# A hybrid decoder layer: transposes of the probabilities ahead of the filling products, later sums of h, and the cache copy in sixteen pieces

## The chip, the cores and the metric

The kernel runs on one core of one Trainium2 chip. The metric is the device time of one execution in microseconds, lower being better; the time of the kernel before is the median of three runs.

## The reference

One decoder layer with three parallel branches is computed in float32 for a prompt of 1024 tokens and, with the same weights, for 8 sample tokens that each have caches. The model's width is 1024.

```python
z = x @ w_in                                   # one projection for all branches and gates
xr, yr, q, k, v, xq, g = jnp.split(z, SPLIT_IDX, axis=-1)
a_out = rg_lru(causal_conv(xr)) * gelu(yr)     # branch a: a linear recurrence
s_out = swa(q, k, v, sinks)                    # branch s: window of 128, 16 query heads, 4 kv heads of 64
c_out = mem_attn(xq, mem_k, mem_v)             # branch c: 256 memory tokens, 4 heads of 256
merged = sum(gates[:, :, n] * (br @ w_branch[n]) for n, br in enumerate((a_out, s_out, c_out)))
h = layer_norm(ALPHA * x + merged @ w_out)
gt, up = jnp.split(h @ w_gate_up, 2, axis=-1)
y = layer_norm(ALPHA * h + (silu(gt) * up) @ w_down)
```

Outputs are y for prompt and samples, the new states of convolution and recurrence, the memory keys and values, and the window caches; the samples' window caches are the old ones shifted by one row, with the new row at the end.

## The kernel before, in words

**Precision.** TensorE multiplies in a reduced float32 format, so each operand is split into a high part, cast on ScalarE (ACT), and a low remainder, subtracted on VectorE (DVE): `split`, lines 80 and 81. A product is then three matmuls (high by high, high by low, low by high; `mm3`, lines 114 to 116) into one PSUM bank. The attention values take two, because there the stationary operand holds both parts side by side.

**Layout and stages.** Activations lie with channels on the 128 partitions and 1032 tokens (1024 and 8) along the free dimension. The tokens are taken in three chunks of 388, 386 and 258 columns (`CH`). In order of time the stages are: `project` (to some 630 us), which computes z by a scheme of seven products in place of eight per pair of weight tiles (`fast_quarter` prepares a weight quarter, `fast_product` multiplies), with the recurrence and the samples' memory attention as side work; `mem_attention` (to some 800 us); `windows` (to some 1030 us); the rest of the branch products and `out_proj` with the first layer norm; `ffn`, whose gate and up products again use the seven products for 20 of 22 column tiles (`gated_step`); and `down` with the second layer norm.

**PSUM.** The eight banks are handed out by tag, two each: `mm`, `s`, `t` and `o`.

**Filling products.** The products of the branches a and c with `w_branch` (tiles `bra` and `brc`, 24 matmuls each) depend on nothing in the attention stages. `fill(1)` traces the next one of them at places chosen by hand, so that TensorE has work while ACT and DVE do a softmax. In `mem_attention` every other half step has a head's key/value projection (`mem_kv`) at that place.

**Window stage.** There are 32 steps, 4 key/value heads by 8 blocks of 128 tokens. `win_scores` makes the scores of four query heads (`bs`, lines 573 and 574, eight matmuls into two banks `s`), masks them and takes the maximum on DVE (line 577), the exponentials on ACT (581), the reciprocal on DVE (582), and multiplies on DVE, POOL and ACT (588 and 586). The values are one step behind: `win_values` of the step before transposes the probabilities on TensorE (`bt`, line 598, four transposes for each of two key blocks), splits the transposed ones (`bph` and `bpl`), multiplies them with the values (`bo`, lines 603 and 604) and stores the result through `bob`. The branch s reads it back later.

**What sets the order.** The program is traced in Python, and a scheduler orders each engine's instructions ahead of time: of those that are ready by its own clock it takes the one that was traced first. Each engine then runs its list in that order and waits at each instruction for what it needs. `issue_after(x)` adds an edge: what is traced in its block on the engine of x is listed behind x. So where a call stands in the source is its priority.

**Sums of h.** For the seven products of `ffn`, `combine` makes sums and differences of blocks of h on DVE and splits them, in three parts for each half of the columns. The last two parts of the second half are traced in phase `ph5b`, beside the weight quarters of the first unit: one part behind the low remainder of the first weight quarter (`last_low`), one behind that of the second.

**Cache copies.** All but one row of the samples' window caches is copied within device memory, 1016 KB for keys and as much for values. Both copies are issued on SyncE's queue (SP) during the seven-product units, behind the weight loads of units 14 and 15. Copies of h back into the residual tiles (516 KB each) are issued in the same way in units 4 to 11. SP issues all DMAs of the kernel.

**First down products.** `down` begins with the two column tiles that were kept on the chip (tile `dk`): eight output tiles, four column ranges each, whose PSUM banks alternate between the tags `mm` and `s`. The last seven-product unit uses the same tags.

Of the kernel before, what the change touches and what calls it, by code (L numbers as in the profile page):

```python
# [18 lines left out]
P = 128  # L19
# [3 lines left out]
NB = 8  # L23
# [7 lines left out]
F_KEPT = (20, 21)  # L31
F_UNITS = F_KEPT + tuple(range(2, 20))
F_DOWN = ((0, 7), (14, 6), (7, 7))
F_CACHE = {8: ("o_swk", "cwk"), 9: ("o_swv", "cwv")}
NORM_AT = (0, 3)
LATE_AT = {4: 2, 5: 3, 6: 5}
CENTER_AT = (2, 4, 5)
# [2 lines left out]
QN = T // 4  # L40
# [19 lines left out]
class Builder:  # L60
# [428 lines left out]
            out.append(p)  # L489
        return out  # L490

    def mem_values(self, h, half, ps, mv):
        nc = self.nc
        pt = [self.bank("t", f"cpt{h}_{half}_{kk}") for kk in range(2)]
        for pr, p in enumerate(ps):
            for u in range(2):
                for kk in range(2):
                    nc.tensor.transpose(pt[kk][:, (pr * 2 + u) * P:(pr * 2 + u + 1) * P],
                                        p[:, u * 256 + kk * P:u * 256 + (kk + 1) * P], self.ident)
        pp = []  # L500
        for kk in range(2):
            hi = self.ph.tile([P, 512], F32R, tag="pt", name=f"cph{h}_{half}_{kk}", bufs=4)
            lo = self.ph.tile([P, 512], F32R, tag="pt", name=f"cpl{h}_{half}_{kk}", bufs=4)
            self.split(hi, lo, pt[kk])
            pp.append((hi, lo))
        for j in range(2):
            o = self.bank("o", f"co{h}_{half}_{j}")
            self.mm3(o, [((mv[kk][0][:, j * P:(j + 1) * P], mv[kk][1][:, j * P:(j + 1) * P]), pp[kk])
                         for kk in range(2)])
            ob = self.ph.tile([P, 512], F32, tag="ob", name=f"cob{h}_{half}_{j}", bufs=2)  # L510
            nc.scalar.copy(ob, o)
            nc.sync.dma_start(self.scr["c"][:, 2 * h + j, half * 512:(half + 1) * 512], ob)

    def mem_attention(self, fill):

        self.load_mem()
        kv = [None] * 4
        fill(6)
        kv[0] = self.mem_kv(0)
        last = None  # L520
        for n in range(8):
            h, half = n // 2, n % 2
            ps = self.mem_scores(h, half, self.mem_queries(h, half), kv[h][0])
            if half == 0 or h == 3:
                fill(1)
            else:
                kv[h + 1] = self.mem_kv(h + 1)
            if last:
                self.mem_values(*last)
            last = h, half, ps, kv[h][1]  # L530
            if n in DEC_AT:
                (self.dec_win_scores, self.dec_win_softmax, self.dec_win_values)[DEC_AT.index(n)]()
        fill(1)
        self.mem_values(*last)


    def win_load(self, kv):
# [50 lines left out]
                (nc.gpsimd if g else nc.vector).tensor_scalar_mul(pg[g], pg[g], r)  # L588
        return pg

    def win_values(self, kv, ops, b, pg):
        nc = self.nc
        nk, vs = len(range(max(b - 1, 0), b + 1)), ops[2]
        ov = self.bank("o", f"bo{kv}_{b}")
        for kk in range(nk):
            pt = self.bank("t", f"bt{kv}_{b}_{kk}")
            for g in range(4):
                nc.tensor.transpose(pt[:, g * P:(g + 1) * P], pg[g][:, kk * P:(kk + 1) * P], self.ident)
            hi = self.ph.tile([P, 512], F32R, tag="pt", name=f"bph{kv}_{b}_{kk}", bufs=4)
            lo = self.ph.tile([P, 512], F32R, tag="pt", name=f"bpl{kv}_{b}_{kk}", bufs=4)  # L600
            self.split(hi, lo, pt)
            v = vs[:, max(b - 1, 0) + kk, :]
            nc.tensor.matmul(ov, v, hi, start=kk == 0, stop=False)
            self.last_mm = nc.tensor.matmul(ov, v, lo, start=False, stop=kk == nk - 1).ins
        for i in range(2):
            ob = self.ph.tile([64, 256], F32, tag="ob", name=f"bob{kv}_{b}_{i}", bufs=4)
            o = ov[:, i * 256:(i + 1) * 256]
            nc.scalar.copy(ob, o[64:128, :])
            nc.vector.tensor_add(ob, o[0:64, :], ob)
            dst = self.scr["s"][:, 2 * kv + i, b * P:(b + 1) * P].rearrange("(e d) t -> d e t", e=2)  # L610
            nc.sync.dma_start(dst, ob.rearrange("p (e t) -> p e t", e=2))

    def windows(self, fill):

        self.mask = self.ph.tile([P, 256], F32, tag="mask", name="mask", bufs=1)
        self.nc.sync.dma_start(self.mask, self.io["cst"][:, P:P + 256])
        nxt, last = self.win_load(0), None
        fill(2)
        for kv in range(4):
            ops = nxt  # L620
            for b in range(8):
                pg = self.win_scores(kv, ops, b)
                if last:
                    fill(1)
                    self.win_values(*last)
                last = kv, ops, b, pg
                if b == 4 and kv < 3:
                    nxt = self.win_load(kv + 1)
        fill(1)
        self.win_values(*last)  # L630

    def product(self, step, br, m, c, wb, gate):

# [564 lines left out]
    def ffn(self, h):  # L1198
        nc, io, tc = self.nc, self.io, self.tc

        def gate_up(f, c, wg, wu):
            t0, n = CH[c]
            pg = self.mm_tile(wg, h, c, f"fg{f}_{c}", tag=("t", "s")[c % 2])
            self.norm_step()
            t = self.ph.tile([P, CW], F32, tag="gt", name=f"ft{f}_{c}", bufs=3)[:, :n]
            nc.scalar.activation(t, pg, AF.Tanh, scale=0.5)
            nc.vector.scalar_tensor_tensor(t, t, 1.0, pg, op0=ALU.add, op1=ALU.mult)
            pu = self.mm_tile(wu, h, c, f"fu{f}_{c}")
            last = nc.vector.tensor_mul(t, t, pu).ins
            nc.sync.dma_start(self.scr["f"][:, f, t0:t0 + n], t)  # L1210
            return last

        st, ts, sums = {}, [], []

        def load(f):
            st[f] = self.fast_load(f"f{f}", io["wgu"][f], io["wgu"][NF + f])
            st[f]["load"]((0, 0), (0, 1), (1, 0), (1, 1))

        todo = [(f, i) for f in F_UNITS for i in range(7)]
        with self.phase("ph5a") as self.ph:  # L1220
            h = self.out_proj(h)
            for f in F_DIRECT:
                wg = self.weights(io["wgu"][f], D, f"wfg{f}")
                wu = self.weights(io["wgu"][NF + f], D, f"wfu{f}")
                for c in range(3):
                    last = gate_up(f, c, wg, wu)
                    if (f, c) in ((0, 1), (1, 0)):
                        with tc.issue_after(self.last_half if f == 0 else last):
                            ts.append({})
                            sums.append(self.combine(f, ts[f]))  # L1230
                            for _ in range(3 - 2 * f):
                                next(sums[f])
        g = [[None] * 3 for _ in range(7)]
        with self.phase("ph5b") as self.ph:
            self.w1 = self.ph
            load(F_UNITS[0])
            for k in range(3):
                self.fast_quarter(st[todo[k][0]], todo[k][1])
                if k < 2:
                    with tc.issue_after(self.last_low):  # L1240
                        next(sums[1])
            for k, (f, i) in enumerate(todo):
                j = k // 7
                if i == 1 and j + 1 < len(F_UNITS):
                    load(F_UNITS[j + 1])
                    if 4 <= j < 12:
                        with tc.issue_after(self.last_load):
                            nc.sync.dma_start(self.M[j - 4], self.scr["h"][:, j - 4, :])
                    if j in (14, 15):
                        name, cache = F_CACHE[j - 6]  # L1250
                        with tc.issue_after(self.last_load):
                            nc.sync.dma_start(io[name][:, 0:P - 1, :], io[cache][:, 1:P, :])
                if k + 3 < len(todo):
                    v, q = todo[k + 3]
                    self.fast_quarter(st[v], q)
                self.gated_step(st[f], i, ts, f)
                if f == F_UNITS[-1] and i in (2, 4, 6):
                    for e in {2: range(4), 4: (4, 5), 6: (6,)}[i]:
                        g[e] = self.load_gated(F_DOWN[0][0] + e, self.S[1][e])
        with self.phase("ph5c") as self.ph:  # L1260
            self.down(g)

    def down(self, g):
# [7 lines left out]
        for m in range(KT):  # L1271
            w = self.weights(io["wdn"][m][:, cols(F_KEPT[0], 2)], 2 * P, f"wdk{m}")
            for th in range(2):
                for p in range(2):
                    ps = self.bank(("mm", "s")[p], f"dk{m}_{th}{p}")[:, :QN]
                    o = HT + QN * p
                    self.mm3(ps, [(w[j], tuple(a[:, o:o + QN] for a in self.S[0][2 * j + th])) for j in range(2)])
                    add(m, HT * th + QN * p, QN, ps)
# [244 lines left out]
```

## Time and profile before

| | before |
|---|---|
| median of 3 runs | 1940.3 us (1939.17 to 1942.13) |
| profiled execution | 1941.22 us |
| its span | 1939.4 us |
| granted TensorE clock | 0.998 |
| TensorE busy, matmuls | 1907.9 us, 98% |
| VectorE busy | 1369.9 us, 71% |
| ScalarE busy | 995.8 us, 51% |
| memory read and written | 194.75 MB and 70.03 MB |

The profile is that of one execution. PE is TensorE's matmuls, PEld its weight loads, which overlap with them; POOL is GpSimd and SP SyncE. A wait is listed under the engine and line that waited and the engine and tile that released it. Rows of the timeline give the start in us, the duration in us, engine, line, operation, and the tiles that it writes and reads; "x8" means that so many rows are merged. The groups give the busy time in us and the mean of one in ns, and behind the second bar the idle time just before.

### The profile page before, as it was taken

The numbers are of one execution on the slowest core, as the hardware profiler recorded it, in microseconds if no ns is written. First come the engines' busy times: TensorE is split into PE (matmuls) and PEld (weight loads), VectorE is DVE, ScalarE is ACT, GpSimd is POOL, SyncE is SP. The second block draws the span as 40 slices with busy tenths as digits, with TensorE's granted clock in tenths as the row PEclk, the third lists the DMA queues.
The fourth block names the chain that finished last, engine by engine and source line by source line (L and its number), as shares of the span: only waits on it lengthen the run. The fifth ranks groups of instructions, "written<-read, shape, count | busy, mean of one in ns | idle before, by whom it ended". The sixth has DMA issues, their size and how long they took to land.

```text
span 1939.4 us, 37218 instructions
## 1 busy us (share of the span) xinstructions
PE 1907.9 (98%) x14245; PEld 1878.5 (97%) x14245; DVE 1369.9 (71%) x2922; ACT 995.8 (51%) x2164; POOL 74.4 (4%) x125
## 2 busy tenths in 40 slices
PE   8999999999999999999999999999999999999997
PEld 8999999999999999988999999999999999999997
DVE  8998889878776655388886558885666656734557
ACT  6666765656665555398774234643333333412224
POOL 0010000100000000021210000000000000000000
PEclk9999999999999999999999999999999999999999
DMA  5554554465233976657525242212333222623202
GB/s 205 179 181 155 172 178 140 159 217 178 80 137 115 304 223 210 166 165 208 148 64 180 88 154 74 94 62 88 110 104 102 101 88 77 186 74 119 83 10 88
DMA packets 154850, 265.14 MB, mean 137 GB/s; under 512 B 18624, under 2 KB 76816, under 8 KB 154640
## 3 DMA queue, kind: packets, MB, share of 16 engines
q1 hardware_dynamic: 154672, 262.76, 42.4%
q8 instruction: 112, 1.84, 0.4%
q14 instruction: 66, 0.54, 0.1%
HBM read 194.75 MB, written 70.03 MB: 137 GB/s over the span
## 4 chain that ended last, share of the span: by engine, by line
PE 84%; ACT 5%; DVE 5%; DMA 4%; issue 2%; SPq 0%; ACTq 0%; DVEq 0%; POOL 0%; POOLq 0%
PE ub L291 4%; PE ub L293 4%; PE ub L292 4%; PE fb L292 4%; PE fb L291 4%; PE fb L293 4%; PE d L115 3%; PE d L116 3%; PE d L114 3%; PE ud L293 2%; PE ud L292 2%; PE ud L291 2%; PE fd L291 2%; PE fd L293 2%; PE fd L292 2%; PE brs L115 2%
## 5 line engine op out<-in xcount | busy, mean ns | idle before, releaser
L581 ACT ACTIVATE bp<-bp,bst 128x257 f32<-128x257 f32 (+1 forms) x128 | 62.7, 493 | 18.2 <-DVE bst L577 18.0
L291 PE MATMUL ub<-th,u_6h 128*128 128x258 f32 x232 | 66.4, 286 | 1.1 <-DVE zb L321 1.1
L293 PE MATMUL ub<-th,u_4l 128*128 128x258 f32 x232 | 65.9, 285 | 0.3 <-DVE u_4l L81 0.3
L291 PE MATMUL ub<-th,u_2h 128*128 128x258 f32 x232 | 66.0, 284 | 0.1
L293 PE MATMUL uc<-th,u_3l 128*128 128x258 f32 x232 | 65.9, 284 | 0.0
L293 PE MATMUL ud<-th,u_1l 128*128 128x258 f32 x232 | 65.9, 284 | 0.0
L293 PE MATMUL ub<-th,u_2l 128*128 128x258 f32 x232 | 65.9, 284 | 0.0
L293 PE MATMUL ud<-th,u_5l 128*128 128x258 f32 x232 | 65.9, 284 | 0.0
L291 PE MATMUL uc<-th,u_3h 128*128 128x258 f32 x232 | 65.7, 283 | 0.0
L293 PE MATMUL ub<-th,u_0l 128*128 128x258 f32 x232 | 65.7, 283 | 0.0
L293 PE MATMUL ub<-th,u_6l 128*128 128x258 f32 x232 | 65.6, 283 | 0.0
L291 PE MATMUL ud<-th,u_5h 128*128 128x258 f32 x232 | 65.6, 283 | 0.0
L291 PE MATMUL ud<-th,u_1h 128*128 128x258 f32 x232 | 65.6, 283 | 0.0
L291 PE MATMUL ub<-th,u_4h 128*128 128x258 f32 x232 | 65.5, 283 | 0.0
L292 PE MATMUL ub<-tl,u_0h 128*128 128x258 f32 x232 | 65.5, 282 | 0.0
L291 PE MATMUL ub<-th,u_0h 128*128 128x258 f32 x232 | 65.4, 282 | 0.0
L292 PE MATMUL ud<-tl,u_1h 128*128 128x258 f32 x232 | 65.3, 282 | 0.0
L292 PE MATMUL ub<-tl,u_2h 128*128 128x258 f32 x232 | 65.3, 282 | 0.0
L292 PE MATMUL uc<-tl,u_3h 128*128 128x258 f32 x232 | 65.3, 282 | 0.0
L292 PE MATMUL ub<-tl,u_4h 128*128 128x258 f32 x232 | 65.3, 282 | 0.0
L292 PE MATMUL ud<-tl,u_5h 128*128 128x258 f32 x232 | 65.3, 282 | 0.0
L292 PE MATMUL ub<-tl,u_6h 128*128 128x258 f32 x232 | 65.3, 281 | 0.0
(828 smaller groups left out, 8052.9 us busy)
## 6 DMA issues: line engine op xcount, KB each, us to landing
ur<-win SPq DMA_DIRECT2D x120, 256.0 KB
urf<-wgu SPq DMA_DIRECT2D x80, 256.0 KB
scr_f<-fo SPq DMA_DIRECT2D x36, 258.0 KB
dck<-cmk SPq DMA_DIRECT2D x32, 256.0 KB
dcv<-cmvT SPq DMA_DIRECT2D x32, 256.0 KB
st<-scr_q SPq DMA_DIRECT2D x32, 256.0 KB
S1L<-scr_f SPq DMA_DIRECT2D x14, 516.0 KB
scr_g<-za SPq DMA_DIRECT2D x12, 516.0 KB
```

The source lines that it names most:

```text
L114: nc.tensor.matmul(ps, sh, mh, start=i == 0, stop=False)
L115: nc.tensor.matmul(ps, sh, ml, start=False, stop=False)
L116: self.last_mm = nc.tensor.matmul(ps, sl, mh, start=False, stop=closes and i == last).ins
L291: mm(sh[:, w], xh, start=opens and k == 0, stop=False)
L292: mm(sh[:, w], xl, start=False, stop=False)
L293: self.last_mm = mm(sl[:, w], xh, start=False, stop=k == 3).ins
L581: nc.scalar.activation(x, x, AF.Exp, bias=st[:, g:g + 1], scale=-1.0, accum_out=st[:, 4 + g:5 + g])
```

## The change

Five things change.

- In `windows`, `win_values` is cut in two. `win_turn` transposes and splits; what is left multiplies and stores. `win_turn` of the step before is traced ahead of `fill(1)`, the rest behind it as now.
- In `mem_attention`, `mem_values` is cut in the same way into `mem_turn` and `mem_values`.
- In `ffn`, both remaining parts of the sums of h are traced behind the low remainder of the second weight quarter.
- The cache copies become sixteen pieces of 127 rows of 256 floats (127 KB), one sample of keys or values each, behind the weight loads of units 3 to 18.
- In `down`, the first products take banks by column half: two in `s`, two in `mm`.

```diff
-F_CACHE = {8: ("o_swk", "cwk"), 9: ("o_swv", "cwv")}
+F_CACHE = (("o_swk", "cwk"), ("o_swv", "cwv"))
...
-    def mem_values(self, h, half, ps, mv):
+    def mem_turn(self, h, half, ps):
         nc = self.nc
         pt = [self.bank("t", f"cpt{h}_{half}_{kk}") for kk in range(2)]
...
             self.split(hi, lo, pt[kk])
             pp.append((hi, lo))
+        return pp
+
+    def mem_values(self, h, half, pp, mv):
+        nc = self.nc
         for j in range(2):
...
             ps = self.mem_scores(h, half, self.mem_queries(h, half), kv[h][0])
+            if last:
+                turned = self.mem_turn(*last[:3])
             if half == 0 or h == 3:
                 fill(1)
             else:
                 kv[h + 1] = self.mem_kv(h + 1)
             if last:
-                self.mem_values(*last)
+                self.mem_values(*last[:2], turned, last[3])
...
+    def win_turn(self, kv, ops, b, pg):
+        nc = self.nc
+        pairs = []
+        for kk in range(len(range(max(b - 1, 0), b + 1))):
             pt = self.bank("t", f"bt{kv}_{b}_{kk}")
             for g in range(4):
                 nc.tensor.transpose(pt[:, g * P:(g + 1) * P], pg[g][:, kk * P:(kk + 1) * P], self.ident)
             hi = self.ph.tile([P, 512], F32R, tag="pt", name=f"bph{kv}_{b}_{kk}", bufs=4)
             lo = self.ph.tile([P, 512], F32R, tag="pt", name=f"bpl{kv}_{b}_{kk}", bufs=4)
             self.split(hi, lo, pt)
+            pairs.append((hi, lo))
+        return pairs
+
+    def win_values(self, kv, ops, b, pairs):
+        nc = self.nc
+        nk, vs = len(pairs), ops[2]
+        ov = self.bank("o", f"bo{kv}_{b}")
+        for kk, (hi, lo) in enumerate(pairs):
             v = vs[:, max(b - 1, 0) + kk, :]
...
                 pg = self.win_scores(kv, ops, b)
                 if last:
+                    turned = self.win_turn(*last)
                     fill(1)
-                    self.win_values(*last)
+                    self.win_values(*last[:3], turned)
...
                 self.fast_quarter(st[todo[k][0]], todo[k][1])
-                if k < 2:
+                if k == 1:
                     with tc.issue_after(self.last_low):
+                        next(sums[1])
                         next(sums[1])
...
-                    if j in (14, 15):
-                        name, cache = F_CACHE[j - 6]
+                    if 3 <= j < 3 + 2 * NB:
+                        name, cache = F_CACHE[(j - 3) % 2]
+                        b = (j - 3) // 2
                         with tc.issue_after(self.last_load):
-                            nc.sync.dma_start(io[name][:, 0:P - 1, :], io[cache][:, 1:P, :])
+                            nc.sync.dma_start(io[name][b, 0:P - 1, :], io[cache][b, 1:P, :])
...
-                    ps = self.bank(("mm", "s")[p], f"dk{m}_{th}{p}")[:, :QN]
+                    ps = self.bank(("s", "mm")[th], f"dk{m}_{th}{p}")[:, :QN]
```

More of the change, by code (lines that the diff above doesn't have):

```diff
@@ L532, in mem_attention @@
                 (self.dec_win_scores, self.dec_win_softmax, self.dec_win_values)[DEC_AT.index(n)]()
+        turned = self.mem_turn(*last[:3])
         fill(1)
-        self.mem_values(*last)
+        self.mem_values(*last[:2], turned, last[3])
     def win_load(self, kv):
@@ L589, in win_scores @@
         return pg
-    def win_values(self, kv, ops, b, pg):
+    def win_turn(self, kv, ops, b, pg):
         nc = self.nc
-        nk, vs = len(range(max(b - 1, 0), b + 1)), ops[2]
-        ov = self.bank("o", f"bo{kv}_{b}")
-        for kk in range(nk):
+        pairs = []
+        for kk in range(len(range(max(b - 1, 0), b + 1))):
             pt = self.bank("t", f"bt{kv}_{b}_{kk}")
@@ L628, in windows @@
                     nxt = self.win_load(kv + 1)
+        turned = self.win_turn(*last)
         fill(1)
-        self.win_values(*last)
+        self.win_values(*last[:3], turned)
     def product(self, step, br, m, c, wb, gate):
```

## The prediction

> **What bounds the kernel now.** I read the page's engine shares first, then the waits of TensorE's weight loads, then the groups of the window stage, then one step of that stage engine by engine. From the page: the engine shares and the granted clock.
>
> ```profile
> PE 1907.9 (98%) x14245; PEld 1878.5 (97%) x14245; DVE 1369.9 (71%) x2922; ACT 995.8 (51%) x2164; POOL 74.4 (4%) x125
> ...
> PEclk9999999999999999999999999999999999999999
> ```
>
> TensorE has work for 98% of the span at full clock, so an edit can only win what TensorE still loses by waiting. The waits of the weight loads (engine, line, what was waited for: us in total, times, longest) say where:
>
> ```profile
> PEld bo L603 <- ACT bph L80: 10.6, 29, 1.1
> ...
> PEld co L114 <- ACT cph L80: 1.3, 5, 0.6
> ...
> PEld fd L291 <- ACT uf_1h L80: 1.2, 1, 1.2
> PEld dk L114 <- DVE fo L1183: 1.0, 1, 1.0
> PEld fb L293 <- DVE uf_0l L81: 1.0, 1, 1.0
> ```
>
> The largest repeated wait is `bo`: the window stage's values product waits for ScalarE's cast of the transposed probabilities. The other four rows are what the rest of the change touches. The groups of the window stage on PE, and the stage's busy times (PE, PEld, DVE, ACT, POOL, clock, DMA share, GB/s), whole and for its first 25 us:
>
> ```profile
> L603 PE MATMUL bo<-bph,vs 128*128 128x512 f32 x60 | 27.1, 451 | 4.1 <-ACT bph L80 3.8
> L604 PE MATMUL bo<-bpl,vs 128*128 128x512 f32 x60 | 24.7, 411 | 0.0
> ```
>
> ```profile
> 825.00:1030.00 205.00, 200.58 (x1279) 184.56 (x1279) 169.91 (x515) 157.67 (x469) 39.58 (x60) 1.00 0.52 145
> 825.00:850.00 25.00, 24.51 (x160) 21.34 (x159) 22.41 (x75) 24.61 (x75) 6.59 (x12) 1.00 0.56 154
> ```
>
> By matmul records TensorE idles 205.0 - 200.6 = 4.4 us here; by weight loads 205.0 - 184.6 = 20.4 us. Which is right decides the size of the gain, and one step of the stage on PE shows it:
>
> ```profile
> 990.09 1.03 PE L598 MATMUL bt<-ident,bp 128*128 128x128 f32 x8
> ...
> 992.77 0.28 PE L574 MATMUL bs<-ks,st 128*128 128x256 f32 x1
> ...
> 995.99 1.03 PE L598 MATMUL bt<-ident,bp 128*128 128x128 f32 x8
> 996.78 0.36 PE L573 MATMUL bs<-ks,st 128*128 128x256 f32 x1
> ...
> 998.04 0.50 PE L603 MATMUL bo<-bph,vs 128*128 128x512 f32 x1 [0.18 <-ACT bph L80]
> 998.38 0.28 PE L574 MATMUL bs<-ks,st 128*128 128x256 f32 x1
> 998.50 0.34 PE L114 MATMUL brc<-S0H,wbc_h 128*128 128x388 f32 x1
> ...
> 999.61 0.40 PE L603 MATMUL bo<-bph,vs 128*128 128x512 f32 x1
> 999.85 0.34 PE L116 MATMUL brc<-S0H,wbc_l 128*128 128x388 f32 x1
> ...
> 1003.46 1.03 PE L598 MATMUL bt<-ident,bp 128*128 128x128 f32 x8
> ```
>
> Eight transposes (995.99), then the next step's scores `bs`, then the first `bo`, then the branch's filling product `brc`. A `bo` that waited holds PE for 998.38 - 998.04 = 0.34 us from start to start, one that did not 999.85 - 999.61 = 0.24. So matmul records overlap, a wait need not show as a gap in them, and a restart costs some 0.1 us besides. I take the weight loads' 10.6, and for the restarts the difference of the two groups' means, 60 x (451 - 411) ns = 2.4: 13.0 us recoverable at most, 0.41 us for each of 32 steps. The Trainium skill ("Perfetto Trace Analysis", section "Identifying the Most-Contended Engine") says that matmul busy share misjudges how near TensorE is to its limit, because matmuls are pipelined, and names the weight loads' busy share instead. Had the matmul row's 3.8 us been all, the sum below would end near 1935 (3.8 x 18/32 = 2.1 in place of 7.3); by the weight loads it ends at 1930. The start-to-start times agree with the page.
>
> **The change, part by part.** (1) Window stage. Now the order traced for step k is scores(k), filling product, then transposes, casts and `bo` of k-1. Transposes to `bo` is a chain of about 1 us that only the next scores cover. Afterwards transposes(k-1) and their casts come ahead of the 24 matmuls of the filling product, and `bo` behind them. No matmul, cast or DMA is added. The cover from transposes to `bo` grows from eight score matmuls to a whole filling product: wide, 998.50 to 1003.46 less three `bo` in between (3 x 0.24) = 4.2 us; the narrow third chunk (258 columns) takes 258/388 of that, 2.8 us.
>
> What it takes away: the transposes of step k now have one filling product between the scores of k and themselves, not two. Behind the end of scores(k) lie 0.79 (eight transposes, 995.99 to 996.78) + 4.2 or 2.8 + four `bo` of 0.24 + eight scores of 0.12 (998.38 to 998.50) = 6.9 us wide or 5.5 us narrow. The softmax must fit in there. How long it takes, by POOL's and ACT's last multiplications of the scores that ended at 992.77 + 0.28 = 993.05:
>
> ```profile
> 996.37 0.93 POOL L588 TENSOR_SCALAR bp<-bp,bst 128x256 f32<-128x256 f32 x1 [4.88 <-DVE bst L582]
> ```
>
> ```profile
> 996.47 0.91 ACT L586 ACTIVATE bp<-bp,bst 128x256 f32<-128x256 f32 x2
> 997.40 0.59 ACT L80 CAST bph<-bt 128x512 fp32r<-128x512 f32 x1
> ```
>
> It ends at 997.38: 4.3 us. Two casts of 0.59 now fall into the same stretch on ACT: 5.5 us. Wide steps keep 1.4 us of room, narrow ones none, so I let the narrow third keep its wait, at the transposes or at `bo`. I do the same for the first five steps, where ACT is busy 24.6 of 25 us and any order waits for it. That is 5 + 27/3 = 14 of 32 steps keeping 0.41 us: 13.0 - 5.7 = **-7.3 us**. The ends: -13.0 if no wait is left; on the other side every transpose waits the longest single wait seen, 1.1 us x 31 = 34, less 13.0: +21. I stay near the first end because the rows give room in two steps of three, and use the far end for a rival. POOL's copy of the sink column waits for the transposes to free its buffer and so comes earlier. The filling product's SP loads keep their order; the stores of `bo`'s results already came behind it.
>
> (2) Memory attention. The same move, with a filling product or a whole key/value projection as cover: the 1.3 us of `co` go, **-1.3** (0 if the key/value copies, now behind these casts on ACT, get later by as much).
>
> (3) Sums of h. The first row below is the last DVE operation of the sums' first part, the second the sum for the second weight quarter, which had to queue behind it:
>
> ```profile
> 1265.74 1.24 DVE L87 SCALAR_TENSOR_TENSOR S1L<-acc,S1H 128x1032 fp32r<-128x1032 f32 x1
> 1266.89 0.68 DVE L276 TENSOR_TENSOR usf<-urf,urf 128x512 f32<-128x512 f32 x1
> ```
>
> That is the 1.2 us wait of `fd`. With both parts behind the second quarter, this wait goes, but the third group of products (`fb` with the moved sums) needs them. Queued behind the added wait on DVE are both parts, some five operations of 1.24 us, and PE needs the first part two groups of 24 matmuls (2 x 24 x 0.12 = 5.8 us) after the unit starts. I take half: **-0.6**, from -1.2 to +1.2.
>
> (4) Caches. SP's issues around the first of the two 1016 KB copies:
>
> ```profile
> 1530.63 11.46 SPq L91 DMA_DIRECT2D urf<-wgu  x4
> 1542.14 0.84 SPq L1252 DMA_DIRECT2D o_swk<-cwk  x1
> 1548.85 21.38 SPq L1190 DMA_DIRECT2D scr_f<-fo  x4
> 1570.32 1.84 SPq L91 DMA_DIRECT2D urf<-wgu  x4
> ```
>
> Behind the copy the next unit's weights are issued 40 us after the last ones, bunched in 1.8 us, and not spread over 11.5; two units on, `fb` waits 1.0 us for a late weight quarter. Sixteen pieces of 127 KB, one per unit, should leave SP's rhythm: **-1.0** (0 at the other end). Fourteen more issues of at most 0.84 us lie on SP, which is no bound.
>
> (5) Banks of the first down products. PE and DVE at the place:
>
> ```profile
> 1672.41 0.28 PE L115 MATMUL dk<-S0L,wdk_h 128*128 128x258 f32 x1
> 1673.52 0.38 PE L114 MATMUL dk<-S0H,wdk_h 128*128 128x258 f32 x1 [0.83 <-DVE fo L1183]
> ```
>
> Two products had run in the two free banks before PE waited for the other two. With the new tags again two run, and then the same release is awaited: **0**, from -1.0 to +1.0.
>
> Sum: -7.3 - 1.3 - 0.6 - 1.0 = -10.2. The profiled execution took 1941.2 us (span 1939.4), 0.9 above the median of 1940.3: 1931.0 for such an execution, and I give **1930** for the median.
>
> **The rivals.** A, the wait only moves: PE runs its queue in order, and if the softmax is late by the order in which ACT takes casts and exponentials, the transposes wait as `bo` did. Then (1) gives 0 and the rest -2.9: 1938. For it: narrow steps have no room. Against: wide ones have 1.4 us.
>
> B, slower: the softmax misses its place in every step. Weight casts, copies of `bo`'s results and the two casts all go ahead of exponentials on an ACT that is busy 157.7 of 205 us; with DVE at 169.9 a chain of 4.3 us can double to 8, against 6.9 and 5.5 of cover. It decides from 0.41 + 2.9/31 = 0.5 us per step on. At 0.9 us for 31 steps: 28 - 13.0 - 2.9 = +12, 1952. Against: the 5.5 us that I count already hold both casts.
>
> C, the pieces hold up weights: each copy runs on few DMA engines, and a weight half issued right behind is late on these. If the 16 units each lose the 0.8 us of the present gap, +13 - 9.2 = +4: 1944. Against: SP leaves 6.7 us (1542.14 to 1548.85) before its next DMA. The Trainium skill ("DMA: Bandwidth & Descriptors", section "Why a DMA increments its semaphore by 16 and not by 1") says that a DMA's number of engines is the largest number up to 16 that divides its slowest dimension, and that 127 partitions get one; no row here shows the engines of a piece.
>
> **How the numbers follow.** Forecast 0.67 (its own range 1924 to 1936), A 0.18 (1936 to 1941), B 0.10, C 0.05. Full recovery, -13.0 - 1.3 - 1.2 - 1.0 - 1.0 = -17.5, is 1923; the upper end takes in A and leaves out B and C. So 1924 to 1941. A measurement tells 0.2% (3.9 us) from no change: faster means under 1936.4. Faster 0.68, of it 0.01 from A; same 0.18 (A, a little of C); slower 0.14.
>
> **What the profile after would show.** Right: the `bo` row of the weight loads' waits under 5 us, no new row of `bt` over 5, the window stage some 7 us shorter, `co`, `fd` and `fb` rows gone, `dk` still there, weight issues every 20 us on SP to the end. Wrong: `bt` waiting for ACT L586, POOL or DVE L588 in most steps (A or B by its sum), or waits of `uf` quarters on DMA (C). What would make it wrong first is the softmax's length under the new order, which no row of before shows.

## The result, and the profile after

The changed kernel takes 1938.87 us, median of 20 runs (1935.71 to 1943.15), against 1940.72 us for the kernel before on the same chip (20 runs, 1939.07 to 1946.49). The ratio is 0.9985, 95% interval 0.9979 to 0.9992, or -2.9 us (-4.1 to -1.6); the two medians lie 1.9 us apart, which is in that interval. By the ratio the change is under the 0.2% that the prediction asked of "faster", and 9 us above its 1930. The profiled execution took 1939.74 us with a span of 1937.9 us; its clock was 0.998 as before.

From the list of waits of TensorE's weight loads, kernel after (engine, tile, line, what it waited for: us in total, times, longest):

```profile
PEld bo L617 <- ACT bph L80: 7.2, 10, 2.5
...
PEld bo L618 <- DVE bpl L81: 3.4, 9, 1.1
...
PEld dk L114 <- DVE fo L1199: 1.3, 1, 1.3
...
PEld fb L292 <- DVE S1L L87: 1.2, 1, 1.2
PEld fd L291 <- ACT uf_1h L80: 1.2, 1, 1.2
...
PEld bt L604 <- ACT bp L593: 1.0, 3, 0.7
...
PEld dk L114 <- DVE acc L1286: 0.7, 1, 0.7
```

From the same list of the kernel before, a row that the prediction does not show:

```profile
PEld bo L604 <- DVE bpl L81: 0.8, 3, 0.3
```

`bo` waits for ScalarE's cast 10 times instead of 29, but its longest wait is 2.5 us where it was 1.1. For the low remainder `bpl`, which VectorE makes from that cast, it waits 9 times instead of 3. `fd` still waits; `fb` now waits for a sum of h; `dk` waits twice. The transposes `bt` wait very little. `co` for ScalarE and `fb` for a late weight quarter are gone.

The window stage by busy times (PE, PEld, DVE, ACT, POOL, clock, DMA share, GB/s; matmuls in brackets), first after, then with the window move alone (run e1 below):

```profile
825.00:1030.00 205.00, 198.87 (x1294) 185.96 (x1293) 170.22 (x518) 159.10 (x471) 37.84 (x61) 1.00 0.53 148
```

```profile
825.00:1030.00 205.00, 202.23 (x1318) 189.00 (x1317) 173.66 (x533) 162.58 (x482) 37.66 (x61) 1.00 0.54 150
```

Before, 1279 matmuls ran in these 205 us; after, 1294; with the window move alone, 1318. So something in the rest of the change seems to take back part of what the window move wins, within the window stage itself; the table below says how much.

To add up stages I use one measure throughout: the time that TensorE lost in a stretch is the sum, over its matmuls, of the time from the start of one to the start of the next, less the median of that for the same shape in that trace. Stretches in us from the span's start, one profiled execution each:

| kernel | 0-825 | 825-900 | 900-1100 | 1260-1280 | 1400-1650 | 1650-1690 | other | all |
|---|---|---|---|---|---|---|---|---|
| before | 14.2 | 7.5 | 9.5 | 1.3 | 1.3 | 1.5 | 3.9 | 39.1 |
| after | 14.0 | 10.3 | 3.5 | 3.3 | 0.3 | 2.0 | 3.9 | 37.4 |
| e1 windows | 16.8 | 6.3 | 4.1 | 1.3 | 1.3 | 1.1 | 4.1 | 35.0 |
| e2 windows, later half | 16.3 | 7.3 | 3.6 | 1.3 | 1.3 | 1.1 | 4.5 | 35.5 |
| e3 memory | 15.1 | 7.6 | 9.5 | 1.4 | 1.2 | 2.1 | 3.9 | 40.7 |
| e4 sums, cast first | 18.7 | 6.2 | 9.3 | 1.8 | 1.3 | 1.8 | 3.8 | 42.9 |
| g4 banks | 15.5 | 6.3 | 9.1 | 1.3 | 1.3 | 2.2 | 3.2 | 38.8 |
| f1 windows, memory | 14.1 | 8.6 | 3.1 | 1.3 | 1.3 | 1.9 | 3.6 | 33.9 |
| f2 all but memory | 14.3 | 6.7 | 3.5 | 3.3 | 0.3 | 3.6 | 3.1 | 34.7 |
| f3 all but sums, banks | 14.1 | 9.8 | 3.3 | 1.3 | 0.3 | 2.0 | 3.6 | 34.5 |
| f4 windows, caches, cast first | 15.7 | 7.4 | 4.0 | 0.9 | 0.3 | 3.6 | 4.4 | 36.2 |
| g1 f4, tangents first | 14.5 | 6.0 | 4.2 | 0.9 | 0.3 | 1.9 | 4.4 | 32.1 |
| h1 g1, gates first | 18.4 | 7.0 | 4.5 | 0.9 | 0.3 | 0.0 | 4.5 | 35.6 |

Before to after: +2.8 in the first third of the window stage, -6.0 in the rest of it, +2.0 at the start of the seven-product units, -1.0 at the end of them, +0.5 at the first down products. The column 0-825 scatters by 5 us between executions, also between kernels whose only differences lie behind it; so one span says nothing about 1 us, while a late column does. In all, the profiled execution after lost 1.7 us less than the one before, near the 1.9 us between the medians.

### The profile page after: what moved, and what is told of

Its sections match the earlier page's. It is cut to its first block, busy times and chain, and to the rows that moved or that the text cites. A ratio compares the mean times of both kernels' runs of the same rounds, so it can differ in the third digit from the quotient of the medians.

```text
span 1937.9 us, 37272 instructions
## 1 busy us (share of the span) xinstructions
PE 1904.7 (98%) x14245; PEld 1878.1 (97%) x14245; DVE 1367.4 (71%) x2922; ACT 996.9 (51%) x2164; POOL 72.7 (4%) x125
## 4 chain that ended last, share of the span: by engine, by line
PE 87%; DVE 4%; DMA 3%; ACT 3%; issue 1%; SPq 0%; ACTq 0%; POOL 0%; DVEq 0%; POOLq 0%
PE ub L293 5%; PE ub L291 5%; PE ub L292 5%; PE fb L292 4%; PE fb L291 4%; PE fb L293 4%; PE d L115 3%; PE d L116 3%; PE d L114 3%; PE ud L293 2%; PE ud L292 2%; PE ud L291 2%; PE fd L291 2%; PE fd L293 2%; PE fd L292 2%; PE brs L115 2%
```

## The experiments

Times are in us by the ratio to the kernel before on the same chip, with the 95% interval of that ratio. The two kernels g2 and g3, further down, leave work out and have one run each; they are not in this table.

| run | change of time |
|---|---|
| e1 windows alone | -6.8 (-9.3 to -4.5) |
| e2 windows, later half of the steps | -7.0 (-9.3 to -4.5) |
| e3 memory attention alone | -1.2 (-2.9 to +0.6) |
| e4 sums, cast first | -0.2 (-1.9 to +1.6) |
| g4 banks alone | +1.0 (-0.6 to +2.7) |
| f1 windows and memory | -3.9 (-5.8 to -1.9) |
| f2 all but memory | -2.9 (-4.7 to -1.2) |
| f3 all but sums and banks | -5.4 (-8.0 to -3.1) |
| f4 windows, caches, cast first | -5.0 (-6.8 to -3.3) |
| g1 f4, tangents first | -8.0 (-10.7 to -5.4) |
| h1 g1, last gates first | -7.4 (-10.1 to -4.9) |

**The parts alone.** e1 is the kernel before with the change of `win_values` and `windows` only. e2 has it for the steps of key/value heads 2 and 3 only:

```diff
-                    turned = self.win_turn(*last)
-                    fill(1)
+                    if kv >= 2:
+                        turned = self.win_turn(*last)
+                        fill(1)
+                    else:
+                        fill(1)
+                        turned = self.win_turn(*last)
```

> Only the window stage's move, the rest as before. Theory E (the early steps): the move gives what was forecast only once branch c's operand is loaded, and loses in the steps beside that load, so the stage alone gives 2 to 4 us; waits of bo on bph of 0.8 to 2.5 us stand between 850 and 900 us and nearly none behind 920. Rival O (the other parts give it back): the stage alone gives 6 to 8 us, and memory attention, sums and down banks of the full change cost 3 to 5.

> The window stage's move for the heads 2 and 3 alone (steps 17 to 32); in the steps before, transposes stand behind the filling product as before. Theory E: no new waits between 850 and 900, and the gain of the later half stays: 5 to 7 us faster than before, so more than the move in all steps. Rival O, and a softmax that is too long everywhere: half the steps give half of what all give, 1 to 4 us, less than e1.

The window move is worth 6.8 us, and the later half of the steps alone as much. By the table the gain lies behind 900 us (9.5 to 4.1 and 3.6). From 825 to 900 us the kernels without the window move lose 7.5, 7.6, 6.2 and 6.3 us, so e1's 6.3 and e2's 7.3 are no gain. Theory E asked for less from e1 than from e2, and falls: when nothing else is moved, moving the early steps costs nothing that can be seen, and gains as little.

e3 is the kernel before with the change of `mem_values` and `mem_attention` only.

> Only the move in memory attention, the rest as before. From the profile of the full change, where waits of dss and dso of some 2 us stand in place of those of co and mv: 0 us, between -1 and +1. By the prediction's term: -1.3 us.

The waits of `co` are gone from its trace, but the time can't be told from before. A new wait stands in the same stage: a key/value product `mv` waits 1.2 us for ScalarE's copy `mvr`. All five kernels with the memory move have this wait (0.9 to 1.2 us), and none of the others. The window stage is as before (7.6 and 9.5).

g4 is the kernel before with the new banks of `dk` only.

> Only the banks of the first down products. The prediction's term: 0, from -1 to +1 us. Theory 0: the wait of dk for DVE fo stays at 0.5 to 1.3 us and a second short wait of dk may appear, together within 1 us of before. Rival: the new order of banks costs 0.6 to 2 us at this place, as the full change and the version without memory attention show it.

No difference that can be measured; `dk` waits for `fo` 0.9 us and for its own sums 0.9 us in two waits (2.2 us lost against 1.5). The rival's 0.6 is within reach of the numbers, so this run does not decide between the two by itself.

**Memory and windows together.** f1 has both moves, f2 is the full change without the memory move, f3 the full change without sums and banks.

> The window move and the memory attention move together; sums, caches and banks as before. Alone the window move gave -6.8 us and the memory move nothing that could be measured; the full change gave -2.9. Theory M: the memory move shifts the start of the window stage so that the early steps' casts of the probabilities fall behind loads of branch c's operand; then this kernel gives -3 to -4.5 us, and its trace shows a wait of bo for ACT of some 2 us between 885 and 900 us. Rival N: the memory move is neutral and the rest of the change gives the time back; then -6 to -8 us, and no wait of bo over 1 us there.

> The full change without its memory attention part. Theory M: the early window steps lose no 2 us, so about -5.5 to -6.5 us (the window move's 6.8, the caches' 1.0, less some 2 that the sums' and the banks' new waits cost). Rival N: the sums and banks give the time back, and it stays at -2.5 to -4 us.

> The full change without its sums and banks parts: windows, memory attention and caches. Theory M: -4 to -5 us, with the 2 us wait of bo near 897 us. Rival N: -7 to -8 us. Under both the wait of fb for S1L near 1272 us is gone and the wait of fd for ScalarE's cast of uf_1h is back at 1.0 us, and fb waits for no late weight quarter near 1610 us.

By their times alone these do not decide: f1 lies where theory M put it, f2 where rival N did, f3 between the two and nearer to M, and the interval of f1 overlaps that of e1. The stretches do. From 825 to 900 us the three kernels with both moves lose 10.3, 8.6 and 9.8 us; those with the window move and without the memory move 6.3, 6.7, 7.4, 6.0 and 7.0 (e1, f2, f4, g1, h1). The difference of the means is 9.6 - 6.7 = 2.9 us. And f2 keeps the loss at the sums (3.3) and lost 3.6 us at the first down products, more than any kernel above it in the table. So f2's time says nothing against a loss of 2.9 us in the window stage: it lost more elsewhere. Both theories hold a part. From the waits of the weight loads in f1, then in e1:

```profile
PEld bo L617 <- ACT bph L80: 6.6, 9, 3.1
```

```profile
PEld bo L610 <- ACT bph L80: 3.4, 8, 0.7
```

The loss has two places. From 860 to 880 us the three kernels with both moves lose 2.0 to 4.1 us (the kernel after most), the five with the window move alone of the two 0.7 to 1.7; from 880 to 900 us it is 2.5 to 3.8 against 1.5 to 2.1. The long wait is in the second. Here it is in the kernel after, on ACT and then on PE:

```profile
889.80 0.51 ACT L80 CAST S0H<-S0L 128x386 fp32r<-128x386 f32 x1
891.12 1.06 ACT L80 CAST S0H<-S0L 128x386 fp32r<-128x386 f32 x2 [0.81 <-DMA S0L<-scr_c]
893.25 0.52 ACT L80 CAST S0H<-S0L 128x386 fp32r<-128x386 f32 x1 [1.08 <-DMA S0L<-scr_c]
893.80 0.37 ACT L622 COPY bob<-bo 64x256 f32<-64x256 f32 x1
894.07 1.35 ACT L80 CAST S0H<-S0L 128x386 fp32r<-128x386 f32 x3
895.32 0.37 ACT L622 COPY bob<-bo 64x256 f32<-64x256 f32 x1
...
896.70 0.58 ACT L80 CAST bph<-bt 128x512 fp32r<-128x512 f32 x1
```

```profile
892.34 1.03 PE L604 MATMUL bt<-ident,bp 128*128 128x128 f32 x8
...
894.79 0.34 PE L114 MATMUL brc<-S0H,wbc_h 128*128 128x386 f32 x1
897.34 0.50 PE L617 MATMUL bo<-bph,vs 128*128 128x512 f32 x1 [2.21 <-ACT bph L80]
```

ScalarE's list has the casts of branch c's operand ahead of the cast of the probabilities. Two rows of them wait for the DMA that reads that operand back (0.81 and 1.08 us), and `bph`, whose transposes do not need it, is late by that. But so it is in f2, which has no such wait of `bo`. The same step there, on ACT and on PE:

```profile
888.99 0.52 ACT L80 CAST S0H<-S0L 128x386 fp32r<-128x386 f32 x1 [0.91 <-DMA S0L<-scr_c]
889.97 0.52 ACT L80 CAST S0H<-S0L 128x386 fp32r<-128x386 f32 x1 [0.47 <-DMA S0L<-scr_c]
...
894.03 0.59 ACT L80 CAST bph<-bt 128x512 fp32r<-128x512 f32 x1
```

```profile
889.14 1.03 PE L597 MATMUL bt<-ident,bp 128*128 128x128 f32 x8
...
891.78 0.39 PE L573 MATMUL bs<-ks,st 128*128 128x256 f32 x1 [0.39 <-DVE bst L577]
...
895.35 0.40 PE L610 MATMUL bo<-bph,vs 128*128 128x512 f32 x1
```

From the first transpose to the cast `bph` it is 896.70 - 892.34 = 4.4 us in the kernel after and 894.03 - 889.14 = 4.9 in f2: 4.2 to 5.0 in the three kernels with both moves, 4.3 to 4.9 in the other five. So the cast is late in all of them. What differs here is TensorE's list: with both moves the first `bo` stands 10 matmuls of `brc` behind the transposes, and without the memory move 22 matmuls, 16 of `brc` and 6 of the next scores. The longer queue covers the late cast, though the scores wait too (0.39 us in the row above).

In the first place ScalarE's list does differ: with both moves the cast `bph` of the step whose `bo` comes near 868 us stands behind five casts of branch c's operand, without the memory move behind four (e1, f2, g1). In the kernel after two of the five wait 1.73 and 1.38 us for the DMA, and `bo` waits 1.2 us for ScalarE and 1.1 for VectorE; in f1 and f3 the casts end sooner and `bo` waits less.

g2 and g3 ask whether the casts are needed for this loss: f1 and e1 without the read and the split of that operand.

```diff
-            self.nc.sync.dma_start(lo.bitcast(F32), self.scr[br][:, k, t0:t0 + n])
-            self.split(hi, lo, lo.bitcast(F32))
+            if br != "c":
+                self.nc.sync.dma_start(lo.bitcast(F32), self.scr[br][:, k, t0:t0 + n])
+                self.split(hi, lo, lo.bitcast(F32))
```

> Windows and memory moved together, and branch c's operand is neither read back nor cast to hi and lo (the products run on what branch a left there). Theory L: the 2 to 3 us wait of bo near 895 us in every kernel with both moves is the cast of the probabilities standing on ScalarE behind casts of that operand which wait for its DMA; without them no bo waits over 0.7 us between 850 and 900 us. Rival P: it comes from the order of the filling products on TensorE alone; then a wait of 1.5 us or more stays.

> The window move alone, with branch c's operand neither read back nor cast: the control for the one before. Both theories: no bo waits over 0.7 us between 850 and 900 us, as with the operand; under theory L the two kernels' stretches from 825 to 900 us need the same time within 1 us, under rival P they differ by 2 us.

From the waits of g2, and then of g3:

```profile
PEld bo L618 <- ACT bph L80: 2.2, 6, 0.5
```

```profile
PEld bo L611 <- ACT bph L80: 2.4, 6, 0.7
```

The long wait is gone, and from 825 to 900 us the two kernels lose 3.9 and 3.8 us (one run each, 1931.1 and 1931.4 us): without these casts the memory move costs the window stage nothing. So the loss needs the late casts, as theory L says. It does not follow that the place of the casts alone makes the difference between f1 and e1. The edit also changed TensorE's list: in g2 and in g3 all 24 matmuls of `brc` stand ahead of `bo` in that step. So these two runs do not test the part of rival P that the rows above show, and a run that changes only the place of `bo` was not made. Which instruction of the memory move changes the lists was not isolated either; it is the scheduler's lists that change, not the work.

**Sums.** The kernel after, at the start of the first unit, on DVE, ACT and PE:

```profile
1264.74 0.68 DVE L276 TENSOR_TENSOR usf<-urf,urf 128x512 f32<-128x512 f32 x1
1266.89 0.69 DVE L81 TENSOR_TENSOR uf_1l<-usf,uf_1h 128x512 fp32r<-128x512 f32 x1 [1.47 <-ACT uf_1h L80]
1267.50 1.23 DVE L1154 TENSOR_TENSOR acc<-acc,acc 128x1032 f32<-128x1032 f32 x1
1268.65 1.23 DVE L81 TENSOR_TENSOR S1L<-acc,S1H 128x1032 fp32r<-128x1032 f32 x1
1269.79 1.22 DVE L1158 TENSOR_TENSOR acc<-acc,acc 128x1032 f32<-128x1032 f32 x1
1270.94 1.23 DVE L87 SCALAR_TENSOR_TENSOR S1L<-acc,S1H 128x1032 fp32r<-128x1032 f32 x1
```

```profile
1264.52 0.38 ACT L1180 COPY fs<-fb 128x258 f32<-128x258 f32 x1 [3.93 <-PE fb L293]
1265.97 0.38 ACT L1180 COPY fs<-fb 128x258 f32<-128x258 f32 x1 [1.08 <-PE fb L293]
1266.24 0.62 ACT L80 CAST uf_1h<-usf 128x512 fp32r<-128x512 f32 x1
...
1268.77 1.07 ACT L86 ACTIVATE S1H<-acc 128x1032 fp32r<-128x1032 f32 x1 [0.34 <-DVE acc L1154]
```

```profile
1266.92 0.39 PE L291 MATMUL fd<-S1H,uf_1h 128*128 128x258 f32 x1 [0.98 <-ACT uf_1h L80]
...
1272.22 0.39 PE L292 MATMUL fb<-S1L,uf_2h 128*128 128x258 f32 x1 [0.99 <-DVE S1L L87]
```

The second quarter's sum is early, as the change meant it. But its cast `uf_1h` stands on ACT behind the copies of the first results (1264.52, 1265.97), and these wait for the products: `fd` waits 0.98 us as before. In the kernel before the cast already stood there, directly behind the second copy:

```profile
1268.27 0.38 ACT L1164 COPY fs<-fb 128x258 f32<-128x258 f32 x1 [1.08 <-PE fb L293]
1268.54 0.62 ACT L80 CAST uf_1h<-usf 128x512 fp32r<-128x512 f32 x1
```

Then both parts of the sums run on DVE, and the difference that `fb` needs (L87) is listed last; its high part (L86) came only at 1268.77: a new wait of 0.99 us. The stretch loses 3.3 us against 1.3. e4 is the sums' change with that cast ahead of the copies:

```diff
-                self.gated_step(st[f], i, ts, f)
+                if k == 0:
+                    with tc.issue_after(st[f]["cast", 1]):
+                        self.gated_step(st[f], i, ts, f)
+                else:
+                    self.gated_step(st[f], i, ts, f)
```

> The later sums of h, and besides the copies of the first unit's first results are listed on ScalarE behind the cast of the second weight quarter; the rest as before. Theory L (ScalarE's list holds the second quarter back, not the sums): the 1.2 us wait of fd goes, and with it the 1.2 us wait of fb for the sums that the full change shows, for DVE starts the sums over 1 us earlier: 1 us faster than before. Rival S (the sums themselves are too long on DVE): fd goes and fb keeps 1 us or more: no change against before.

`fd` waits no more and `fb` still does, 1.2 us, as rival S had it (1.8 us lost). Two lists set this place, ACT's and DVE's, and the change left `fd` its wait and gave `fb` a new one.

**A version from these findings.** f4 is the window move, the cache pieces, and the cast ahead of the copies, with the sums in the order of before.

> A version made from what the runs showed: the window move and the caches in pieces; the sums stay in the order of before, but ScalarE copies the first unit's first results only behind its cast of the second weight quarter; memory attention and banks as before. All theories: -6.8 for the windows, -1.0 for the caches, -0.7 to -1.0 for the wait of fd, so -8 to -9 us against before, which would be 5 to 6 us under the full change. Its trace should show neither fd's wait for ACT L80 nor fb's for DVE L87.

Its time, -5.0, misses the -8 to -9. `fb`'s wait is gone and `fd`'s is down to 0.3 us (0.9 us lost), the caches give their 1.0, but the first down products lose 3.6 us. On ACT and PE at that place, in f4:

```profile
1665.61 1.05 ACT L80 CAST S1H<-S1L 128x1032 fp32r<-128x1032 f32 x1 [2.08 <-DMA S1L<-scr_f]
1666.57 0.41 ACT L1187 ACTIVATE ft<-fs 128x258 f32<-128x258 f32 x1
```

```profile
1668.99 0.39 PE L114 MATMUL dk<-S0H,wdk_h 128*128 128x258 f32 x1 [1.96 <-DVE fo L1192]
```

The wait carries VectorE's name, and is a DMA's lateness: a tangent of the last unit stands on ACT behind the cast of a chunk that is read back, its gate `fo` comes later, and the bank of `dk` with it. g1 lists the tangents ahead of two of these casts:

```diff
+                if f == F_UNITS[-1] and i == 5:
+                    with tc.issue_after(self.last_tanh):
+                        for e in (4, 5):
+                            hi, lo = self.S[1][e]
+                            self.split(hi, lo, lo.bitcast(F32))
```

> As the version with the window move, the caches in pieces and the cast ahead of the first copies, and besides the last unit's two hyperbolic tangents on ScalarE come ahead of its casts of two gated chunks that are read back (S1H, waiting for DMA S1L<-scr_f). Theory D: the wait of dk for DVE fo (2.2 us in that version, 0.8 to 1.7 in others) is that DMA's lateness, passed on because ScalarE's list has the casts first; then the wait falls to 0.8 us or less, whatever the DMA does, and the time is 1 to 2 us under that version, -6 to -8 against before. Rival R: the products fd and their vector operations set it; then the wait stays at 0.8 to 2.2 us.

The time is in the range of theory D, -8.0, but the wait stayed at 1.5 us, which rival R asked for. In g1, on DVE:

```profile
1663.72 1.23 DVE L81 TENSOR_TENSOR S1L<-S1L,S1H 128x1032 fp32r<-128x1032 f32 x1
1665.65 1.24 DVE L81 TENSOR_TENSOR S1L<-S1L,S1H 128x1032 fp32r<-128x1032 f32 x1 [0.70 <-ACT S1H L80]
1666.80 0.42 DVE L1192 SCALAR_TENSOR_TENSOR fo<-fo,fb 128x258 f32<-128x258 f32 x1
```

The tangents are on time now, and the same lateness comes through VectorE's list. h1 also lists the casts of all three late chunks behind the tangents, and these differences behind the first sums of the down products:

```diff
+            if m in (0, 1, 2):
+                hi, lo = self.S[1][4 + m]
+                with self.tc.issue_after(self.last_add):
+                    nc.vector.tensor_sub(lo, lo.bitcast(F32), hi.bitcast(F32))
```

> As the version with the tangents first, and besides VectorE's differences of the three gated chunks that are read back (S1L, behind casts that wait for DMA S1L<-scr_f) stand behind the last unit's gates fo and behind the first down products' sums. With the tangents first the wait of dk for DVE fo stayed at 1.5 us, and the trace showed the second fo on VectorE behind two of these differences, one of which waited 0.70 us for its cast. Theory D: this wait is the DMA's lateness passed on by VectorE's order; then no dk waits over 0.4 us and the time falls by 1 us or more against that version. Rival R: the products set it; then a wait of 0.8 us or more stays.

On ACT in h1:

```profile
1672.45 1.06 ACT L1279 CAST S1H<-S1L 128x1032 fp32r<-128x1032 f32 x1 [2.78 <-DMA S1L<-scr_f]
```

This is the cast of the last chunk, which waits for its DMA in every kernel (0.5 to 2.8 us). Here nothing of TensorE waits for it, no row of `dk` is left among the waits, and the stretch loses 0.0 us. So with the banks of before the wait of `dk` is this order, and neither the banks nor the products. The whole time, -7.4, is level with g1's: the 1 us that theory D asked for besides can't be seen in it. g1 and h1 are the fastest versions: ratios 0.9959 and 0.9962, against 0.9985 for the full change.

How long a cast waits also depends on when ScalarE comes to it. From the issue of two of these reads on SP to the cast of the second of their chunks it was 5.7 us in e1 (1660.28 to 1665.93) and 7.2 in f4 (1658.46 to 1665.61). With the whole cache copies it was 5.7 to 6.1 us in eight kernels and 6.9 in a ninth (g3), with the pieces 6.4 to 8.0 in five. So the pieces may make this read later; no run has the pieces alone, and the cause stays open.

## Why the prediction was wrong, step by step

- **(1) Windows, -7.3: right alone, -6.8** (17.0 to 10.4 us by the table, -6.6). The composition was not right. A dozen or so early steps up to 900 us, not five, gain hardly anything: five kernels in which these steps are as before lose 6.2 to 7.6 us there, the five with the window move alone of the two 6.0 to 7.4. Behind 900 us the table gives -5.4. The narrow steps keep a wait, as allowed for, but for VectorE's low remainder (0.3 to 0.5 us in four of e1's steps), and most of the wide ones keep none. That the total came so near is in part luck. By the weight loads' 13.0 us the sum was sized well; the matmul rows' 3.8 us would have made it 2.1. Here the rule of the Trainium skill ("Perfetto Trace Analysis", "Identifying the Most-Contended Engine") agrees with the run: -6.8 alone.
- **(2) Memory attention, -1.3: the step that failed.** I costed it as if its effect ended with its stage. There the waits of `co` went, and the wait of `mv` for ScalarE's copy `mvr` came, the end at 0 that I had named; alone, its -1.2 can't be told from nothing. With the window move it cost the window stage 2.9 us: it changed the lists of ScalarE and TensorE there, so that TensorE came to `bo` before casts that stand behind a late read. The prediction counted the instructions that move; it looked neither at the casts on ACT that wait for a DMA nor at how few matmuls of TensorE's list would be left to cover them.
- **(3) Sums, -0.6, from -1.2 to +1.2: +2.0, outside; the second step that failed.** The one row that I read (the sum queued behind L87) was not what ended the wait: in the kernel before, too, the cast stood on ACT behind the copies, and it would have kept the wait of `fd` without that queue. "I take half" for the two parts had no row behind it; the trace shows a whole new wait of 0.99 us and a restart.
- **(4) Caches, -1.0: right in its own stretch.** In every kernel with pieces the stretch loses 0.3 us, in every one without 1.2 or 1.3. From SP in the kernel after:

```profile
1590.65 11.69 SPq L91 DMA_DIRECT2D urf<-wgu  x4
1602.39 0.52 SPq L1270 DMA_DIRECT2D o_swk<-cwk  x1
...
1610.67 11.86 SPq L91 DMA_DIRECT2D urf<-wgu  x4
```

The weights are issued every 20 us, and a piece takes 0.52 us of the queue. Rival C's late weights did not come, and neither did its premise: the trace has each piece as 16 packets.
- **(5) Banks, 0: alone +1.0 (-0.6 to +2.7), not settled.** With the old banks what decides the place is the order behind the DMA.

The sum by what the runs gave, window move -6.8, its loss with the memory move +2.9, sums +2.0, caches -1.0, is -2.9, the measured change, with memory's own stage and the banks left at nothing. That it agrees to the digit is luck: the interval of e1 alone is 4.8 us wide, and what the memory move does ahead of 825 us is lost in the scatter of that column. Of the 7.3 us between forecast and result, 4.2 are in (2), 2.6 in (3) and 0.5 in (1). Rival A gave 1938, near the result, but for a reason that did not come: `bt` waits some 2 us in all (1.0 for ACT is its largest row), and the window move does what it says.

## What to carry to other kernels

In this kernel, where each engine runs a fixed list in order, a wait on a DMA was passed to whatever is listed behind it, under another engine's name; follow a wait back until the releaser did not itself wait. How much of it TensorE then loses depends on how many matmuls of its own list stand ahead of the one that waits. When a group is moved, compare the lists of both engines, and put what waits for a DMA behind what TensorE needs next. Check any cause found in a slow kernel against the same step of a fast one: here the late cast stood in both. Parts that are right alone need not add: 6.8 us became 3.9 with a part that by itself did nothing that could be measured, though the intervals of these two overlap.

## What was not expected of the hardware

The same read of 516 KB can land at very different times at one place of nearly the same program: from its pair's issue to its cast it was 5.7 us in e1, 7.2 in f4 and 8.0 in g1. Its own issue comes 1.4 us after the first of the pair (f4), so it landed some 4 to 7 us after its issue, while the profile of f4 gives a median of 3.6 us for these reads. A DMA's median time to landing is thus no bound to plan an order by.

The pieces of 127 rows are not slow. From the DMA issues of the kernel after (KB each, median us from issue to landing), the lower two rows the pieces, the upper two transfers of 128 KB:

```profile
dsk<-cwkT SPq DMA_DIRECT2D x8, 128.0 KB, 2.3
dsv<-cwv SPq DMA_DIRECT2D x8, 128.0 KB, 2.8
o_swk<-cwk SPq DMA_DIRECT2D x8, 127.0 KB, 2.6
o_swv<-cwv SPq DMA_DIRECT2D x8, 127.0 KB, 2.7
```

A piece lands as fast as those. The Trainium skill ("DMA: Bandwidth & Descriptors", "Why a DMA increments its semaphore by 16 and not by 1") would give a DMA over 127 partitions one engine. That case does not arise here: the two sides of a piece are contiguous memory without partitions, and the trace has each piece as 16 packets of 8,128 bytes that start within 0.3 to 1.4 us. The whole copies of before went as 16 packets of 65,024 bytes, the first eight together and the other eight over 2 us later, and each packet took 2.4 to 4.0 us.
